# Chunked attention in a streaming-encoder layer: bias matmuls on 64 rows, four probability buffers, a new order of scores and products

## The chip, the cores and the metric

One Trainium2 chip, all 8 cores. Each core computes half of one of the four sequences of the batch; even cores run one program (half 0), odd cores the other (half 1). The metric is the device time of the slowest core, in microseconds (us). A core has a matmul engine (TensorE, "PE" in the profile, with its weight loads "PEld"), VectorE (DVE), ScalarE (ACT), GpSimd (POOL) and a queue engine (SP). The granted clock is the share of its full clock that TensorE got. Some executions fall in a slow state, in which cores of a die run at a lower clock.

## The reference, cut to what matters

```python
x = x + 0.5 * swiglu(rmsnorm(x), ffn1)            # feed-forward, width 2816
z = rmsnorm(x) @ w_in                             # q, k, v (8 heads of 64), conv input (2 x 512)
# chunk of 64 queries attends to its own chunk and the 8 before it (576 keys)
s = einsum(q, k) / 8 + rel_bias[clip(distance)]   # masked where the chunk is out of the band
attn_out = softmax(s) @ v
conv_out = silu(layernorm(depthwise_conv(glu(u))))
x = x + concat(attn_out, conv_out) @ w_out
x = x + 0.5 * swiglu(rmsnorm(x), ffn2)
y = rmsnorm(x)
```

x is 4 x 4096 x 1024. The scores are held transposed: keys on the partitions (tiles of 128), queries on the columns. The bias is constant for far keys, so only a band of at most 256 queries per key tile needs a table; the same table carries the mask (-30000).

## The kernel before

The kernel is generated by Python: a scheduler inside it models the time of each engine at build time, picks the next ready piece of work for TensorE, and writes out a fixed order for every engine. An attention *unit* is one head pair (two heads, `e` = 0 and 1) over some key tiles, 1024 or fewer score columns in two PSUM banks. Scores and bias of a unit:

```python
for (r, a, w, o_) in u["lst"]:            # scores: two heads, 64 contraction rows each
    for e in range(2):
        ops.append((e, kslice(...), qT[e * 64:e * 64 + 64, j, ...], o_, w, ...))
for (r, a, w, o_) in u["lst"]:            # bias and mask: identity (128 x 128) times a table
    for e in range(2):
        if r >= 3:
            ops.append((e, ident, cb[:, tb:tb + hi - lo], o_ + lo - a, hi - lo, ("cb",), None))
        if r < nt:
            ops.append((e, ident, mask0, o_ + r * 128 - a, 128, ("cb",), None))
...
pi = nxt("Pb", 2)                         # two probability buffers
act(Pb[:, pi, :, 0:w], src, AF.Exp, 2 * w, ...)
```

The products take V and a block of ones as weights (128 rows, 64 columns), into an output bank and a sum bank. After the last unit of a head pair, ScalarE makes 1/sum by Ln and Exp, and VectorE multiplies. The loop, one unit of scores ahead of the products, with a fresh bank pair for each head pair:

```python
qk(units[0])
for i, u in enumerate(units):
    if i + 1 < len(units):
        yield rdy1
        qk(units[i + 1])
    yield fn            # P ready, and two free banks if this is the head pair's first unit
    pv(u)
    if u["last"]:
        fin1(u)         # Ln, Exp, later the multiply
```

Where the scheduler expects TensorE to wait 0.8 us or more it inserts dummy matmuls ("fillers", 256 columns into a free bank), to keep its clock up:

```python
n = int((gap - 0.3) / (0.25 if P.t["pe"] < 9 else 0.125))
for i in range(n):
    P.op("pe", lambda h: h.matmul(o, lhsT=onesS, rhs=cb[:, B_ONES:B_ONES + 256], ...), 0.118, ...)
```

The softmax here doesn't subtract the row's maximum and nothing guards it: scores larger than these inputs give would overflow.

## Time and profile before

| | before |
|---|---|
| time, median of the first 4 runs (one of them slow) | 1403.45 us |
| spans of the cores in the profile | 1394.2 to 1401.2 us, granted clock 0.992 to 0.997 |
| TensorE busy, core 0 | 1355.6 us, 97% |
| attention on core 0, two windows | 97.7 + 98.4 us |
| half 0: matmuls, form changes, fillers | 9310, 251, 140 |

How to read the profile here: start times of matmuls are exact, but durations overlap, since matmuls are pipelined. The list of groups shows it for the bias (columns: name, shape, count, busy us, mean ns):

```profile
L484 PE MATMUL psA<-cb_sb 128*128 128x128 bf16 x192 | 22.7, 224 | 0.0
L484 PE MATMUL psA<-cb_sb 128*128 128x256 bf16 x88 | 17.5, 281 | 0.0
```

A bias matmul of 128 columns has a mean of 224 ns, yet the next one of the same form starts 56 ns later. What one costs is the distance from start to start, and the cost of an order shows where that distance exceeds what the width explains.

### The profile page before, as it was taken

The page shows a single profiled execution, that of the slowest core. Times are in us where ns is not written, and L with a number is a line of the kernel's source. Part 1 is how long each engine was busy: PE and PEld are TensorE (multiplying, and loading weights), DVE is VectorE, ACT ScalarE, POOL GpSimd, SP SyncE. Part 2 cuts the span into 40 slices and gives each one's busy share as a digit, 9 for nine tenths or more (in the row PEclk, how much of TensorE's full clock was granted, in tenths as well). Part 3 has the DMA queues.
Part 4 walks back from the last instruction along what each step waited for, and adds up shares of the span by engine and source line. Part 5 has one row for each costly group of instructions (what it writes and reads, how often), then busy time and mean ns, then how long its engine had stood idle before and what let it go on. Part 6 is the DMA issues. An engine that isn't in the chain of part 4 may idle for free.

```text
span 1401.2 us, 25261 instructions; the slowest of 8 cores (1394.2 to 1401.2 us)
## 1 busy us (share of the span) xinstructions
PE 1355.6 (97%) x9310; PEld 846.8 (60%) x9310; DVE 484.9 (35%) x906; ACT 444.7 (32%) x839; POOL 255.2 (18%) x302
## 2 busy tenths in 40 slices
PE   7999999999999999999999999999998999999995
PEld 3575566556554565665565766666664467666654
DVE  3332222452643332222365222225344333222225
ACT  3410011342566631001246100225338663100123
POOL 0155000522123120000062000014041201000012
PEclk9999999999999999999999999999999999999998
DMA  8479144136181443243547544452354406244503
GB/s 192 105 145 197 36 80 87 31 98 146 51 163 28 112 73 69 53 87 51 111 140 241 106 77 90 72 96 65 98 125 92 91 2 121 48 78 87 106 1 123
DMA packets 34032, 132.13 MB, mean 94 GB/s; under 512 B 3440, under 2 KB 11760, under 8 KB 26096
## 3 DMA queue, kind: packets, MB, share of 16 engines
q0 software_dynamic: 17856, 93.48, 35.3%
q1 hardware_dynamic: 16048, 36.96, 8.3%
q8 instruction: 78, 1.28, 0.4%
q14 instruction: 50, 0.41, 0.1%
HBM read 196.37 MB, written 18.09 MB: 153 GB/s over the span
## 4 chain that ended last, share of the span: by engine, by line
PE 89%; ACT 3%; DMA 3%; DVE 2%; issue 2%; DVEq 0%; POOL 0%; ACTq 0%; SPq 0%; POOLq 0%
PE psA L484 52%; PE ps L484 37%; ACT dreg L494 2%; DMA ring<-wgu 2%; DVE hT L714 1%; DVE dreg L714 1%; DMA xres<-xin 1%; DVE xres L885 1%; ACT L492 1%; DMA yout<-dreg 0%; DVE dreg L984 0%; PE ps L472 0%; DVEq L240 0%; ACT scr L492 0%; POOL ring L583 0%
## 5 line engine op out<-in xcount | busy, mean ns | idle before, releaser
L484 PE MATMUL psA<-hT,ring 128*128 128x256 bf16 (+2 forms) x4608 | 718.3, 317 | 5.4 <-DVE hT L714 1.8
L484 PEld LDWEIGHTS psA<-hT,ring 128*128 128x128 bf16 x4608 | 449.5, 98 | 269.7 <-issue 15.3
L494 ACT ACTIVATE dreg<-psA 128x512 f32<-128x512 f32 (+5 forms) x372 | 210.9, 573 | 693.9 <-PE psA L484 688.0
L484 PE MATMUL ps<-at,ring 128*128 128x256 bf16 (+2 forms) x2112 | 327.2, 317 | 0.5 <-DVE xres L885 0.5
L855 DVE TENSOR_TENSOR at<-psA,dreg 128x256 bf16<-128x256 f32 (+2 forms) x264 | 141.5, 536 | 485.6 <-PE psA L484 417.5
L484 PEld LDWEIGHTS ps<-at,ring 128*128 128x128 bf16 x2112 | 206.4, 98 | 119.2 <-issue 0.9
L885 DVE SCALAR_TENSOR_TENSOR xres<-ps,xres 128x256 f32<-128x256 f32 (+2 forms) x192 | 101.8, 533 | 194.4 <-PE ps L484 194.0
L662 POOL TENSOR_TENSOR ssum<-ssum,sq 128x256 f32<-128x256 f32 (+2 forms) x114 | 107.1, 940 | 216.2 <-ACT sq L494 213.3
L583 POOL DMA_DIRECT2D ring<-wgu x45 | 27.7, 616 | 419.1 <-PE psA L484 195.7
L484 PE MATMUL ps<-dreg,ring 128*128 128x256 bf16 (+3 forms) x672 | 97.0, 301 | 0.2 <-DMA ring<-cwscr 0.2
L494 ACT ACTIVATE sq<-xres 128x256 bf16<-128x256 f32 (+2 forms) x115 | 58.0, 511 | 97.8 <-DVE xres L885 64.2
L484 PEld LDWEIGHTS ps<-dreg,ring 128*128 128x128 bf16 x672 | 65.5, 98 | 27.6 <-issue 0.9
L714 DVE SCALAR_TENSOR_TENSOR hT<-xres,cs_sb,rstd 128x256 bf16<-128x256 f32 (+2 forms) x120 | 70.0, 636 | 16.8 <-ACT rstd L494 16.8
L484 PE MATMUL ps<-hT,ring 128*128 128x256 bf16 (+2 forms) x384 | 61.6, 317 | 0.1
L484 PEld LDWEIGHTS ps<-hT,ring 128*128 128x128 bf16 x384 | 37.1, 98 | 21.2 <-issue 0.3
L484 PE MATMUL ps<-dreg,at 128*64 128x256 bf16 (+3 forms) x264 | 35.0, 280 | 12.5 <-ACT dreg L494 12.3
L492 ACT ACT_TABLE_LOAD x36 | 46.2, 1283 | 0.7
L484 PE MATMUL ps<-dreg,cb_sb 128*64 128x256 bf16 (+5 forms) x314 | 42.7, 283 | 1.4 <-DVE dreg L763 1.1
L1356 DVE TENSOR_TENSOR xres<-ps,xres 128x256 f32<-128x256 f32 (+2 forms) x48 | 25.7, 535 | 31.6 <-PE ps L484 31.3
L494 ACT ACTIVATE dreg<-dreg 128x256 f32<-128x256 f32 (+6 forms) x52 | 26.6, 511 | 30.1 <-DVE dreg L984 27.5
L484 PE MATMUL psA<-cb_sb 128*128 128x128 bf16 (+1 forms) x280 | 35.5, 242 | 0.0
L1375 POOL TENSOR_TENSOR dreg<-cmp_sb,cb_sb 128x2304 bf16<-128x2304 bf16 x8 | 32.3, 4042 | 12.9 <-DMA cwscr<-dreg 12.3
(73 smaller groups left out, 568.4 us busy)
## 6 DMA issues: line engine op xcount, KB each, us to landing
ring<-wgu POOLq DMA_DIRECT2D x43, 1024.0 KB, 8.9
ring<-wdA POOLq DMA_DIRECT2D x16, 768.0 KB, 8.8
ring<-wdB POOLq DMA_DIRECT2D x16, 640.0 KB, 6.8
ring<-cwscr POOLq DMA_DIRECT2D x16, 576.0 KB, 5.9
cwscr<-dreg SPq DMA_DIRECT2D x8, 576.0 KB, 9.9
ring<-wab POOLq DMA_DIRECT2D x8, 512.0 KB, 7.6
ring<-wout POOLq DMA_DIRECT2D x4, 1024.0 KB, 9.7
yout<-dreg SPq DMA_DIRECT2D x2, 2048.0 KB, 6.9
```

What stands on the lines that cost most here:

```text
L484: P.op("pe", lambda h: h.matmul(o, lhsT=lhsT, rhs=rhs, start=start, stop=stop, skip_group_check=True), (max(n / 2400.0 + 0.0025, 0.03) if ...
L492: P.op("act", lambda h: h.activation(out=scr[0:1, i:i + 1], in_=onesS[0:1, 0:1], func=func), 1.5, ("cb1",), ())
L494: P.op("act", lambda h: h.activation(out=out, in_=in_, func=func, **kw), 0.12 + n / 1200.0 + (0.09 * sum(isinstance(v, bass.AP) for v in k ...
L583: P.dma("pool", lambda h, dst=dst, src=src: h.dma_start(out=dst, in_=src), wtok(p, i), (256 if p.reads else 512) * w, reads=p.reads, after ...
L662: pool(lambda h: h.tensor_tensor(out=ss, in0=ss, in1=sqt, op=ALU.add), n, (sk, ("sq", i)), (sk,))
L714: dve(lambda h, dst=dst, xin=xin, gcol=gcol: h.scalar_tensor_tensor(out=dst, in0=xin, scalar=gcol, in1=rt, op0=ALU.mult, op1=ALU.mult), n, ...
L855: dve(lambda h, at=at, ub=ub, tt=tt: h.tensor_tensor(out=at, in0=ub, in1=tt, op=ALU.mult), n, (("ps", bU), ("tmpF", ti)), (("AT", gi, fl, ...
L885: dve(lambda h, xo=xo, bk=bk: h.scalar_tensor_tensor(out=xo, in0=bk, scalar=0.5, in1=xo, op0=ALU.mult, op1=ALU.add), n, (("ps", b), xk), ( ...
L1356: dve(lambda h, xo=xo, bk=bk: h.tensor_tensor(out=xo, in0=bk, in1=xo, op=ALU.add), n, (("ps", b), xk), (xk,))
L1375: P.op("pool", lambda h, o_=o_, i0=i0: h.tensor_tensor(out=o_, in0=i0, in1=i1, op=ALU.mult), 4.1, ("cmp", "cb"), (("cwb", i % 2),))
```

## The change

Intent: make TensorE's attention work cheaper and let it run further ahead of ScalarE. Four things change together. (1) The bias is multiplied as two halves of 64 table rows, with 64-row identity windows, so both heads of a pair run side by side in the array form of the scores. (2) Four probability buffers instead of two, up to four units open, and a loop that picks scores or products one at a time. (3) One output and sum bank pair for the whole attention of a group, instead of a fresh one per head pair; the other two banks stay free for projections. (4) The conv's squares are kept in place and summed in one run of 16 matmuls. The rest is memory moved about to make room; for that, the ones of the sum products share a block that holds 1/1024, which Ln undoes by a scale of 1024.

```diff
-                            for e in range(2):
-                                hh = 2 * j + e
-                                if r >= 3:
-                                    ...
-                                    ops.append((e, ident, cb[:, tb:tb + hi - lo], o_ + lo - a, hi - lo, ("cb",), None))
-                                if r < nt:
-                                    ops.append((e, ident, mask0, o_ + r * 128 - a, 128, ("cb",), None))
+                            parts = []
+                            if r >= 3:
+                                q0 = (r - 4) * 128
+                                for half_, lim in ((0, 192), (1, 256)):
+                                    lo, hi = max(a, q0), min(a + w, q0 + lim)
+                                    parts.append((half_, B_BT + j * BW + 192 * half_ + lo - q0, o_ + lo - a, hi - lo))
+                            if r < nt:
+                                parts.append((0, B_M0, o_ + r * 128 - a + 64, 64))
+                            for half_, tb, c_, w_ in parts:
+                                for e in range(2):
+                                    z = B_ID + 64 * (1 - half_)
+                                    ops.append((e, cb[64 * e:64 * e + 64, z:z + 128], cb[64 * e:64 * e + 64, tb:tb + w_],
+                                                c_, w_, ("cb",), w_ / 4800.0 + 0.0025))
 ...
-                        pi = nxt("Pb", 2)
+                        pi = nxt("Pb", 4)
 ...
-                        if u["bi"] == 0:
-                            del ob[:]
-                            for e in range(2):
-                                ob.append(fb_take())
-                                mode["lru"].remove(ob[e])
 ...
-                    qk(units[0])
-                    for i, u in enumerate(units):
-                        ... (the loop above)
+                    def qk_at():
+                        if a == N or a - c > 3:
+                            return INF
+                        ...
+                    while c < N:
+                        fn = lambda: min(qk_at(), pv_at())
+                        yield fn
+                        while True:
+                            lim = ...
+                            if pv_at() <= lim and units[c]["last"]:
+                                pv(units[c]); fin1(units[c]); c += 1
+                            elif qk_at() <= lim:
+                                qk(units[a]); a += 1
+                            elif pv_at() <= lim:
+                                pv(units[c]); ...; c += 1
+                            else:
+                                break
```

(The first products of a head pair now wait until the multiply of the one before has read the single bank pair.)

## The prediction

> **What bounds the kernel now.** I read the page's engine shares first, then the chain that ended last, then the sums of waits, then two stretches of the timeline.
>
> ```profile
> PE 1355.6 (97%) x9310; PEld 846.8 (60%) x9310; DVE 484.9 (35%) x906; ACT 444.7 (32%) x839; POOL 255.2 (18%) x302
> PE 89%; ACT 3%; DMA 3%; DVE 2%; issue 2%; DVEq 0%; POOL 0%; ACTq 0%; SPq 0%; POOLq 0%
> ```
>
> TensorE sets the end: it is busy 97% of the span and is 89% of the chain. Most of that is the two feed-forward layers, which the change doesn't touch. Only TensorE time saved, or TensorE waits shortened, can move the result. Attention runs twice on a core, once per group of blocks; on core 0 its matmuls lie at 370 to 468 us and 1049 to 1147 us. Two windows around them, and the list of TensorE's waits:
>
> ```profile
> 370.00:468.00 98.00, 92.26 (x798) 49.21 (x797) 49.33 (x78) 67.55 (x103) 19.93 (x18) 1.00 0.36 69
> 1048.00:1147.00 99.00, 90.91 (x874) 51.20 (x873) 42.35 (x74) 72.83 (x112) 17.30 (x16) 0.98 0.32 65
> ```
>
> ```profile
> PE ps L484 <- ACT dreg L494: 13.0, 28, 3.0
> PE ps L472 <- DVE dreg L763: 7.0, 1, 7.0
> ```
>
> The columns of the windows are length, then PE, PEld, DVE, ACT and POOL busy. ScalarE is 69% and 74% busy here, against 32% over the span, and 13.0 us of TensorE's waits are the product with V waiting for the exponential. So in attention ScalarE is the second limit. The pipeline itself, TensorE then ScalarE:
>
> ```profile
> 393.96 0.39 PE L484 MATMUL psA<-dreg,at 64*128 64x512 bf16 x2
> 394.28 0.39 PE L484 MATMUL psA<-cb_sb 128*128 128x256 bf16 x2
> 394.61 0.30 PE L484 MATMUL ps<-dreg,at 128*64 128x256 bf16 x2
> 394.74 0.28 PE L484 MATMUL ps<-dreg,cb_sb 128*64 128x256 bf16 x2
> 394.95 0.39 PE L484 MATMUL psA<-dreg,at 64*128 64x384 bf16 x4
> ```
>
> ```profile
> 1082.02 0.41 PE L484 MATMUL ps<-dreg,at 128*64 128x512 bf16 x2 [0.20 <-ACT dreg L494]
> 1089.34 0.41 PE L484 MATMUL ps<-dreg,at 128*64 128x512 bf16 x2 [0.19 <-ACT dreg L494]
> ```
>
> ```profile
> 1082.90 0.50 PE L484 MATMUL psA<-cb_sb 128*128 128x256 bf16 x4
> 1083.50 1.02 ACT L494 ACTIVATE dreg<-psA 128x1024 bf16<-128x1024 f32 x1 [0.71 <-PE psA L484]
> 1084.82 1.02 ACT L494 ACTIVATE dreg<-psA 128x1024 bf16<-128x1024 f32 x1 [0.29 <-PE psA L484]
> 1086.05 1.02 ACT L494 ACTIVATE dreg<-psA 128x1024 bf16<-128x1024 f32 x1 [0.20 <-PE psA L484]
> ```
>
> In the first of these three, the start times matter: the durations of matmuls overlap. A unit of attention runs in three array forms: scores (64 rows by 128), bias (128 by 128, an identity as the weights), products and sums (128 by 64). The score pair of 512 columns holds TensorE from 393.96 to 394.28, 0.32 us, where 512 columns take 0.216 us between equal forms. I took the distances from start to start of all matmuls of core 0: with the same form after it, a full-array matmul of 128, 256, 512 columns holds the array 56, 109, 216 ns (medians); with another form after it, 152, 205, 312 ns. So each change of form costs 96 ns at every width. The last two fences are one head pair in a stretch with nothing else to run: it takes 7.32 us, and ScalarE, itself nearly full, still idles 0.71 + 0.29 + 0.20 us waiting for scores, because only one unit of scores is computed ahead.
>
> **What the Trainium skill says.** "TensorEngine Tiling (Array Packing)", Key Properties: changing the tiling mode drains the engine, changing only the tile does not. The trace agrees, 96 ns a change. The same page's Performance Considerations allow two-fold row tiling when the contraction is 64 or less; the score pairs show it (two matmuls of 64 rows start 3 to 4 ns apart and share one stream time). "TensorE: Matmul & The Clock Gate", Back-to-back issue gap: N/2.4 + 2.5 ns when warm; 56, 109 and 216 ns agree. The same section says that small matmuls stop getting shorter at about 25 ns each; the kernel before has no matmul under 128 columns, so no trace of it shows this, and the change adds 64-column ones.
>
> **The change, part by part.** Counts below are from the order of the two built programs; half 0 is the program of cores 0, 2, 4, 6, half 1 of the odd cores.
>
> Fewer form changes. The bias now uses 64-row matmuls, the same form as the scores, and the new order issues several units of scores and of products in a row. Changes of form fall from 251 to 156 in half 0 and from 240 to 140 in half 1: 95 x 0.096 = 9.1 us and 100 x 0.096 = 9.6 us less.
>
> Bias work. Before, half 0 has 280 bias matmuls on the full array, 192 of 128 and 88 of 256 columns: 192 x 0.056 + 88 x 0.109 = 20.3 us. After, there are 456, in 228 pairs (two heads side by side): 72 pairs of 64 columns, 68 of 128, 44 of 192, 44 of 256. Score pairs followed by score pairs in the trace take 64 ns at 128 and 117 ns at 256 columns, so about N/2.4 + 10. That gives 72 x 0.037 + 68 x 0.064 + 44 x 0.090 + 44 x 0.117 = 16.1 us, 4.2 less. The 37 ns is extrapolated; at the 50 ns of two issue floors it would be 0.9 us more, so I count 3.2 us saved (half 1: 19.9 to 15.1, counted as 3.8).
>
> Keep-warm fillers. The program puts dummy 256-column matmuls where its schedule expects TensorE to wait 0.8 us or more. They run whether or not the wait comes. Half 0 goes from 140 to 204, half 1 from 214 to 271, all the new ones in attention: 64 x 0.109 = 7.0 us and 57 x 0.109 = 6.2 us more. This is the sign that a good part of the saved TensorE time becomes waiting for ScalarE.
>
> Other waits. I summed, over each attention stretch of core 0, what the start-to-start distances exceed width plus form change: 7.4 and 11.6 us, fillers not counted; on core 1, 4.9 and 9.8 us. Scores may now run up to four units ahead (four probability buffers instead of two), score and product matmuls are picked one unit at a time, and the output projection of a finished block is spread between units instead of coming as one burst of 64 matmuls. In the lonely stretch the 1.2 us of ScalarE idling per head pair should fall. Against it: the output and sum banks were a fresh pair per head pair and are now one pair for all, so the first product of a head pair waits for Ln (0.59 us), Exp (0.63) and the multiply (0.69) of the one before. I put the net at 6 us less of 19.0 in half 0 and 5 less of 14.7 in half 1; this is a judgement, not a sum.
>
> Moved only. The 16 matmuls of the conv's squares per group stand together at the end instead of between; same form, same columns. Exponentials, Ln and evictions keep their counts and sizes. Smaller tables in the setup lie before TensorE needs them.
>
> Sum, half 0: -9.1 - 3.2 + 7.0 - 6 = -11.3 us; half 1: -9.6 - 3.8 + 6.2 - 5 = -12.2 us. The even cores were the slower, so 1403.45 - 11.3 = 1392; as the interleaving may well give more than I dared in the judged term, I say 1391.
>
> **The rivals.** First, ScalarE is the true bound of attention, and all TensorE time saved comes back as waits for the exponential. For it: 72.83 us of ScalarE in the second window, and the added fillers. Against it: outside the lonely stretches TensorE had projections to run, and was busy 91 to 92 of 98 to 99 us. It would leave 1400 to 1404. Second, the single output pair puts Ln, Exp and multiply, about 1.9 us, on the path at each of the 24 head pairs of half 0 (six blocks of four). With 1 us exposed at half of them, 12 us eat the gain: about 1403. Against it: up to three units of exponentials can be ready meanwhile. Third, the overlap works fully: form changes and bias save 12.3 us, fillers only replace waits, and 12 of the 19 us of waits go: about 1384. Fourth, 64-column pairs or their weight loads cost far more than 37 ns; at 100 ns, 72 x 0.063 = 4.5 us are lost.
>
> **Range and chances.** The certain part (changes of form, bias) is 12 to 13 us; fillers and waits can add or remove about 10. So 1380 to 1400 should hold it 8 times in 10. Two per cent is 28 us, down to 1375.4; that needs the certain part and nearly all of attention's waits, which ScalarE's load forbids: 0.04. A loss over 2% would need waits doubled: 0.01.
>
> **What would show it.** Right: form changes at 96 ns each still, 95 fewer; bias groups as 64*128 forms whose pairs follow each other in 40 to 120 ns; both attention windows of core 0 shorter by 4 to 8 us each, the rest of the span unchanged within 1 us; ScalarE's share in them higher, up to 80%. Wrong: fillers followed by waits of over 1 us at the start of each head pair (the second rival); bias pairs of 64 columns spaced over 60 ns; or waits on ScalarE adding up to over 20 us. If the time falls but the feed-forward stretches changed, my account of the cause is wrong even where the number is right.

## The result, and the profile after

The changed kernel takes 1387.21 us (median of 10 runs) against 1404.67 us (median of 15 runs of the kernel before, slow ones included in both medians). The ratio of the fast runs is 0.9886, 95% interval 0.9875 to 0.9897: some 16 us less. A ratio here is the mean time of one kernel's fast runs over that of the other's of the same rounds, so it is not quite the ratio of the medians. Spans by core are 1377.4 to 1382.6 us in the profile. On a second chip, as a control for later runs, it measured 1387.14 against 1402.90, ratio 0.9893 (0.9880 to 0.9906).

The page of the changed kernel, engine shares and chain by engine:

```profile
PE 1342.8 (97%) x9550; PEld 849.4 (61%) x9550; DVE 484.6 (35%) x901; ACT 447.6 (32%) x847; POOL 256.5 (19%) x302
PE 85%; DMA 6%; ACT 3%; DVE 2%; issue 2%; POOL 0%; SPq 0%; DVEq 0%; ACTq 0%; POOLq 0%
```

TensorE is as busy in share, with 240 more matmuls and 12.8 us less busy time. The two attention windows of core 0, in the columns of the windows shown in the prediction:

```profile
368.00:454.00 86.00, 84.15 (x892) 48.29 (x890) 43.83 (x68) 68.06 (x106) 18.90 (x17) 1.00 0.42 78
1040.00:1129.00 89.00, 86.12 (x1017) 54.40 (x1016) 39.41 (x66) 71.61 (x112) 17.15 (x16) 1.00 0.35 73
```

From the first score matmul to the end of the last product, attention went from 97.7 and 98.4 us to 85.2 and 87.4, so 12 and 11 us less, with about the same ScalarE work in the windows (68.06 and 71.61 us, against 67.55 and 72.83), so ScalarE is busy 79% and 80% of them. The matmuls that were three forms per unit, now from the timeline of TensorE:

```profile
403.36 0.39 PE L482 MATMUL psA<-dreg,at 64*128 64x256 bf16 x4
403.59 0.38 PE L482 MATMUL psA<-cb_sb 64*128 64x64 bf16 x6
403.90 0.35 PE L482 MATMUL ps<-dreg,at 128*64 128x384 bf16 x2
```

The four scores (two pairs of 256 columns) hold the array 0.23 us and the bias follows with no change of form. The six bias matmuls, 512 columns per head, hold it 0.31 us: 0.213 of streaming and one change of 0.096. And three lines of the list of TensorE's waits over the span:

```profile
PE psA L482 <- DVE hT L712: 4.0, 5, 1.0
PE ps L482 <- DVE dreg L1283: 2.0, 6, 0.6
PE psA L482 <- ACT dreg L492: 1.1, 3, 0.4
```

The line of 13.0 us, products waiting for the exponential, is gone from the list. Two others stand there: the first product of a head pair waits for the multiply of the one before (L1283, 2.0 us), and, after attention, the second feed-forward waits for its normalised input (L712; 4.0 us, 1.8 before).

To split the result I took the two attention windows of core 0 (first score matmul to the end of the last product) apart. Projections, attention work, form changes and fillers are counted from the order of the built program and multiplied by the spacings of the trace: columns/2.4 + 2.5 ns for a full-array matmul, columns/4.8 + 3 ns for one of a side-by-side pair, 96 ns for a change of form, 109 ns for a filler. Counting from the built order matters, since the traces of some cores lack about 100 matmul records. Waits are the rest of the window, so they include what is lost while the granted clock is low.

| core 0, us | windows | projections | attention work | form changes | fillers | waits | rest of the span and projections |
|---|---|---|---|---|---|---|---|
| before | 196.1 | 75.4 | 71.0 | 23.9 (249) | 4.7 | 21.1 | 1280.5 |
| after | 172.6 | 73.6 | 65.8 | 14.8 (154) | 11.7 | 6.7 | 1283.7 |
| difference | | | -5.2 | -9.1 | +7.0 | -14.4 | +3.2 |

The sum is -18.5 us; the span of core 0 fell by 18.6. On core 1 the same terms are -5.8, -9.6, +6.3, -9.2 and -0.7: -19.0, and its span fell by 18.9.

Part of these waits is a lower clock. After the longest wait of the kernel before, the trace has a stretch of 3.4 us at half clock (the third column from the right), in which TensorE is busy throughout:

```profile
1073.26 0.41 PE L484 MATMUL ps<-dreg,at 128*64 128x512 bf16 x2 [2.96 <-ACT dreg L494]
1073.83:1077.24 3.41, 3.41 (x26) 1.57 (x24) 0.00 (x0) 1.23 (x2) 0.00 (x0) 0.50 0.48 124
```

Half of it, 1.7 us, is an estimate of what it cost; it sits in the 21.1 us of waits, and the windows of the changed kernel have no such stretch. So the gain has a small share that comes by way of the clock.

### The profile page after: what moved, and what is told of

The parts are those of the page before. It is cut to its first block, busy times and chain, and to the rows that moved or that the text cites. A ratio compares the mean times of both kernels' runs of the same rounds, so it can differ in the third digit from the quotient of the medians.

```text
span 1382.6 us, 25718 instructions; the slowest of 8 cores (1377.4 to 1382.6 us)
## 1 busy us (share of the span) xinstructions
PE 1342.8 (97%) x9550; PEld 849.4 (61%) x9550; DVE 484.6 (35%) x901; ACT 447.6 (32%) x847; POOL 256.5 (19%) x302
## 3 DMA queue, kind: packets, MB, share of 16 engines
q0 software_dynamic: 17856, 93.48, 36.2%
## 4 chain that ended last, share of the span: by engine, by line
PE 85%; DMA 6%; ACT 3%; DVE 2%; issue 2%; POOL 0%; SPq 0%; DVEq 0%; ACTq 0%; POOLq 0%
PE psA L482 51%; PE ps L482 34%; DMA ring<-wgu 3%; ACT dreg L492 1%; DVE dreg L712 1%; DVE hT L712 1%; DMA xres<-xin 1%; DMA ring<-wv 1%; ACT L490 1%; ACT pb L492 1%; DMA yout<-dreg 0%; DMA ring<-cwscr 0%; DMA dreg<-gscr 0%; DVE xres L883 0%; DVE dreg L1283 0%
## 5 line engine op out<-in xcount | busy, mean ns | idle before, releaser
L492 ACT ACTIVATE dreg<-psA 128x256 f32<-128x256 f32 (+4 forms) x330 | 173.6, 530 | 670.6 <-PE psA L482 662.6
L492 ACT ACTIVATE sq<-xres 128x256 bf16<-128x256 f32 (+2 forms) x115 | 57.8, 511 | 98.4 <-DVE xres L883 64.9
L712 DVE SCALAR_TENSOR_TENSOR hT<-xres,cs_sb,rstd 128x256 bf16<-128x256 f32 (+2 forms) x120 | 73.4, 660 | 5.2 <-ACT rstd L492 5.2
L492 ACT ACTIVATE dreg<-dreg 128x288 bf16<-128x288 f32 (+8 forms) x84 | 40.3, 480 | 59.6 <-DVE dreg L1111 29.4
L492 ACT ACTIVATE pb<-psA 128x1024 bf16<-128x1024 f32 (+2 forms) x42 | 37.6, 911 | 3.9 <-PE psA L482 3.9
L1393 POOL TENSOR_TENSOR dreg<-pb 128x2304 bf16<-128x2304 bf16 x8 | 32.2, 4040 | 4.7 <-DMA cwscr<-dreg 4.2
L470 PE MATMUL ps<-cb_sb 128*128 128x256 bf16 x204 | 26.6, 283 | 6.3 <-issue 6.3
L482 PE MATMUL ps<-ring,hT 128*128 128x512 bf16 x136 | 30.9, 379 | 0.6 <-DMA ring<-wv 0.6
```

The costliest lines, as they stand in the source:

```text
L482: P.op("pe", lambda h: h.matmul(o, lhsT=lhsT, rhs=rhs, start=start, stop=stop, skip_group_check=True), (max(n / 2400.0 + 0.0025, 0.03) if ...
L492: P.op("act", lambda h: h.activation(out=out, in_=in_, func=func, **kw), 0.12 + n / 1200.0 + (0.09 * sum(isinstance(v, bass.AP) for v in k ...
L712: dve(lambda h, dst=dst, xin=xin, gcol=gcol: h.scalar_tensor_tensor(out=dst, in0=xin, scalar=gcol, in1=rt, op0=ALU.mult, op1=ALU.mult), n, ...
L1393: P.op("pool", lambda h, o_=o_, i0=i0: h.tensor_tensor(out=o_, in0=i0, in1=i1, op=ALU.mult), 4.1, ("cmp", "i32", "cb"), (("cwb", i % 2),))
```

## The experiments

Two theories. A: TensorE's work is what counts, so cheaper bias and fewer changes of form are the gain. B: attention is paced by the exchange between TensorE and ScalarE, so TensorE time saved alone comes back as waiting, and the deeper order is the gain. Part (3), the single bank pair, is a suspect for a loss. Every run below gave a correct result unless said otherwise, and its ratio is to the kernel before on the same chip. Every edit makes the generator write a new fixed order, with another number of fillers; so a run tests an edit with the order that comes of it, not the edit alone.

**1. The new bias alone, in the kernel before** (bias_only).

```diff
 # kernel before; loop, two probability buffers and bank pairs unchanged
-    ops.append((e, ident, cb[:, tb:tb + hi - lo], ...))       # full array
+    ops.append((e, cb[64*e:64*e+64, z:z+128], cb[64*e:64*e+64, tb:tb+w_], ...))   # 64 rows, two halves
```

> The kernel before with the new bias alone (64-row bias matmuls and tables); old attention loop, two probability buffers, output pair per head pair. Built order: form changes 251 to 188 in half 0, 240 to 181 in half 1; fillers 140 to 172 and 214 to 291. Theory A (TensorE work is what counts: 63 x 0.096 = 6.0 us of form changes and about 4.5 us of bias time come off in full): ratio to before 0.992 to 0.993, some 10 us less. Theory B (ScalarE limits attention, so TensorE time saved alone returns as waits on the exponential): ratio 0.997 to 1.000, and the sum of TensorE's waits on ScalarE plus fillers grows by 6 us or more over the 13.0 us and 43 attention fillers of before.

Measured: 1398.97 against 1402.25 us, ratio 0.9979 (0.9967 to 0.9992). Theory A asked for 0.992 to 0.993 and falls; B's range holds. On core 0 attention work and form changes fell by 11.2 us together, but fillers and waits together rose from 25.8 to 31.8 us. Its list of waits, where before it was 13.0 us:

```profile
PE ps L481 <- ACT dreg L491: 14.5, 24, 3.5
```

TensorE is ready sooner and waits longer for the same exponential. Over half of the saving is given back. (Core 0's span fell by 6.9 us, the time of the slowest core by only 3: the other even cores have clocks of 0.990 to 0.992 here, against 0.992 to 0.994 before.)

**2. The old bias in the changed kernel** (old_bias). The bigger tables leave room for three probability buffers only, so its control is run 3.

```diff
 # changed kernel with three probability buffers
-    ops.append((e, cb[64*e:64*e+64, z:z+128], cb[64*e:64*e+64, tb:tb+w_], ...))
+    ops.append((e, ident, cb[:, tb:tb + hi - lo], ...))
```

> The changed kernel with the old full-array bias (identity weights, one matmul per head and key tile), new attention loop and one output pair; for want of memory three probability buffers instead of four, so it is to be compared with three_p. Form changes 233 and 223. Theory A (form changes and bias time are the gain): at most 2 to 4 us of the 16 us remain, ratio 0.997 to 0.999. Theory B (overlap by the new loop is the gain): 10 us or more remain, ratio 0.990 to 0.993.

Measured: 1396.18 us, ratio 0.9956 (0.9940 to 0.9971), some 6 us less than before: between the two expectations. So the loop alone (with the single bank pair and the conv's squares, which stay in) is not the gain either. It did do what B says to the waits: in core 0's attention, fillers and waits fell from 25.8 to 14.8 us, and the exponential is no longer waited for by products.

```profile
PE ps L485 <- DVE dreg L1282: 2.2, 4, 0.8
PE psA L485 <- ACT dreg L495: 1.4, 3, 0.7
```

**3. Three probability buffers** (three_p), the control of run 2.

```diff
-                        pi = nxt("Pb", 4)
+                        pi = nxt("Pb", 3)
-                        if a == N or a - c > 3:
+                        if a == N or a - c > 2:
```

> The changed kernel with three probability buffers and at most three open units instead of four; the control for old_bias. Form changes 168 and 160, fillers 201 and 281. If the fourth buffer matters little: ratio to before 0.989 to 0.991 (the changed kernel has 0.9886). If depth is the gain: 0.993 or more.

Measured: 1385.47 us, ratio 0.9881 (0.9866 to 0.9896), the same as with four. No worth of the fourth buffer shows. Now the two halves can be added up: bias alone -0.21%, loop without the new bias -0.44%, together -1.19%. Part (4), the conv's squares, was not run alone. The parts are worth more together than apart. In the old loop the new bias saved 11.2 us of core 0's TensorE work and gave 6.0 of them back as idle time; in the new loop (runs 2 and 3) it saved 11.5 and gave back 2.7.

**4. Two probability buffers** (two_p).

```diff
-                        pi = nxt("Pb", 4)
+                        pi = nxt("Pb", 2)
-                        if a == N or a - c > 3:
+                        if a == N or a - c > 1:
```

> The changed kernel with two probability buffers and at most two open units, as before. Form changes 198 and 185, fillers 307 and 332, that is 103 and 61 more fillers than in the changed kernel (11 and 7 us). Theory B: with the single output pair and no depth, the chain Ln, Exp, multiply is exposed at each head pair, ratio 0.998 to 1.004. Theory A: only 42 form changes come back (4 us), ratio 0.991 to 0.993.

Measured: 1405.06 us, ratio 1.0022 (1.0008 to 1.0035). The whole gain is gone, though bias and most of the saved form changes are still there. As theory B said, the wait that replaces the exponential is the multiply of the head pair before, through the single bank pair:

```profile
PE ps L482 <- DVE dreg L1283: 6.3, 12, 1.0
PE ps L482 <- ACT dreg L492: 3.0, 9, 0.5
```

With the fillers that stand in those waits (22.9 us), core 0's attention idles 36.2 us, more than before the change (25.8) and twice as much as with three buffers (17.5, from runs 2 and 3).

**5. The single bank pair alone, in the kernel before** (one_pair).

```diff
 # kernel before
-                        if u["bi"] == 0:
-                            ... take two free banks
-                            mode["lru"] += b2          # given back after the multiply
+                    # one pair taken at the start of the group's attention; the first products of a
+                    # head pair wait for the multiply of the one before (cut; their priority rule goes too)
```

> The kernel before with one output and sum bank pair for all head pairs, as in the changed kernel, and nothing else; one unit of scores ahead as before. Built order: fillers 140 to 265 and 214 to 296 (125 and 82 more, 13.6 and 8.9 us). If the single pair is a cost that only depth hides: attention windows longer, ratio 1.004 to 1.010. If the single pair is free (it leaves two banks to other work): 0.998 to 1.001.

Measured: 1406.85 against 1402.03 us, ratio 1.0035 (1.0020 to 1.0051), just under the range expected of a cost. Taken alone the single pair loses some 5 us; a wait that the list of the kernel before doesn't have appears:

```profile
PE ps L484 <- DVE dreg L1291: 4.9, 9, 0.8
```

So this part of the change is a cost. As far as the lists of waits tell, the depth hides most of it, and 2.0 us of it, plus fillers, are left in the changed kernel. That is not shown by a run of its own: a version with depth and two bank pairs was not tried, since with four of the eight banks holding scores and four outputs, none is left for the projections that fill TensorE.

**6. No fillers in attention** (no_fill).

```diff
-                if gap < 0.8 or gap > 100 or "cb1" not in P.lastw:
+                if gap < 0.8 or gap > 100 or "cb1" not in P.lastw or attention_is_running:
```

> The changed kernel without fillers in attention (half 0: 204 to 97). If fillers only stand in waits: the removed 107 x 0.109 = 11.7 us come back as waits on ScalarE and the ratio to before stays 0.987 to 0.990. If fillers overshoot the waits and delay work: 0.983 to 0.986. If the waits without them let the granted clock drop: more half-clock stretches and 0.990 to 0.994.

Measured: 1390.95 us, ratio 0.9914 (0.9899 to 0.9929), slower than the changed kernel by 0.3% (by 0.2%, with intervals that overlap a little, if its second measurement, 0.9893, is taken; neither was on this chip). The fillers stand in waits: without them core 0's waits are 20.5 us, against 6.7 + 11.7 with them. The list of waits says on what, and the list of cores why it is slower:

```profile
PE ps L483 <- DVE dreg L1284: 7.0, 7, 1.8
PE psA L483 <- ACT pb L493: 3.7, 2, 3.5
```

```profile
core 1: 1386.6 us, clock 0.990
core 7: 1384.3 us, clock 0.990
```

In the changed kernel these two cores had clocks of 0.997 and 0.995. Over all fast runs the cores have 0.989 to 0.994, against 0.993 to 0.998 in the changed kernel. The gaps bring stretches of half clock, as the third reading said. On core 1 one of 10 us surrounds the end of a wait for an exponential that stands behind the Silu block:

```profile
423.25 0.42 PE L483 MATMUL ps<-dreg,vh 128*64 128x256 bf16 x2 [6.19 <-ACT dreg L493]
421.00:431.00 10.00, 6.84 (x56) 3.77 (x58) 0.69 (x1) 7.99 (x10) 0.00 (x0) 0.51 1.03 183
```

On core 0, 6.8 us of attention run at half clock, so some 3.4 of the 20.5 us are that and not waiting. The run also shows what the changed kernel really waits for: the multiply (7.0 us), and score banks behind the Silu block on ScalarE (3.5 us in one wait).

**7. No Ln and Exp of the sums, in the changed kernel** (no_ln). The result is wrong (relative error 0.035): the multiply uses a constant.

```diff
-                        act(rs[:, ri, 0:n], bank(b2[1])[:, 0:n], AF.Ln, n, ..., scale=1024.0)
-                        act(rt, rt, AF.Exp, n, (("rs", ri),), (("rs", ri),), scale=-1.0)
...
-                            dve(lambda h: h.tensor_tensor(out=o_, in0=i0, in1=rt, op=ALU.mult), n, ...)
+                            dve(lambda h: h.tensor_scalar(out=o_, in0=i0, scalar1=1.0 / 600, ...), n, ...)
```

> The changed kernel without Ln and Exp of the softmax sums (24 x 1.2 us less for ScalarE and a chain shorter by as much); wrong result on purpose, the multiply uses a constant. Theory B (waits on ScalarE are what is left in attention): the 11.6 us of fillers and 6.7 us of waits of core 0 fall by 6 to 10 us, ratio to before 0.981 to 0.985. If attention is TensorE-bound already: 0.987 to 0.989.

Measured: 1377.01 us, ratio 0.9815 (0.9800 to 0.9830), 0.7% under the changed kernel: as expected of waits on ScalarE (across chips: the changed kernel was not run on this one). Fillers and waits of core 0 fall from 18.4 to 8.8 us. The run takes away both ScalarE's load and the chain to the multiply, and does not tell these two apart.

**8. The same removal in the kernel before** (no_ln_before), wrong as well.

> The same removal in the kernel before; wrong result on purpose. With two output pairs and one unit ahead, if its waits come from ScalarE's load: 5 to 9 us less, ratio 0.994 to 0.996. If they come from the order (TensorE waits for the one exponential in flight, whatever else ScalarE does): ratio 0.997 to 1.000.

Measured: 1386.50 against 1402.03 us, ratio 0.9889 (0.9874 to 0.9904). This is far more than either reading expected. The products' wait for the exponential, 13.0 us in the kernel before, is nearly all gone:

```profile
PE ps L484 <- ACT dreg L494: 1.6, 5, 0.7
```

The list of the kernel before has no wait for the multiply, so it is ScalarE's work on Ln and Exp that made the products wait for the exponential; whether by its amount or by its place in the queue, the run does not tell. The gain is as large as that of the change, but it is not the same 16 us: run 7 shows that the removal is still worth some 10 us on top of the change, so only about 6 of the 16 us are common to both (an estimate: 16 + 16 alone, 26 together).

**9. The changed kernel again, and a candidate beyond it** (after_again, silu_once, sq_dve, sq_silu, on one chip). Run 6 showed a wait behind the Silu of the conv's norm. They run as two blocks of eight, each with a table load before and after it; one block of 16 saves two loads. The other edit moves the squares of the third norm to VectorE while attention runs.

```diff
 # silu_once
-                    if grp % 8 == 0:
-                        yield lambda: max(P.est("act", (("acc", grp + 7),)) - 0.2, P.t["act"] - 1.0)
+                    if grp == 0:
+                        yield lambda: max(P.est("act", (("acc", 15),)) - 0.2, P.t["act"] - 1.0)
 # sq_dve: during attention
-                act(sqt, xin, AF.Square, n, ...)
+                dve(lambda h: h.tensor_tensor(out=sqt, in0=xin, in1=xin, op=ALU.mult), n, ...)
```

> The changed kernel itself, unedited, on the same chip as the next three, as their control: ratio to before 0.988 to 0.990.

> The changed kernel with the 16 Silu of the conv norm in one run instead of two runs of eight with two exponentials between: two table loads of 1.28 us and their dummy fewer per group on ScalarE. If ScalarE's load in attention is what is left: 21 and 39 fillers fewer, 2 to 4 us less, ratio to before 0.985 to 0.987. If the longer block of Silu (about 8 us without an exponential) starves TensorE: 0.989 or more.

> The changed kernel with the squares for the third norm on VectorE instead of ScalarE while attention runs (about 11 us per group off ScalarE, VectorE was about half busy). These squares come late, where the output projection already fills TensorE, and the count of fillers does not change (206, 271): if only the load in the lonely stretch counts, ratio to before 0.987 to 0.990, no gain; if ScalarE's load counts everywhere in attention: 0.981 to 0.985.

> Both edits together, the candidate for a better version: as silu_once by the first reading (0.985 to 0.987), 0.980 to 0.983 if both count.

| | median, us | ratio to before | 95% interval |
|---|---|---|---|
| after_again | 1387.14 | 0.9893 | 0.9880 to 0.9906 |
| silu_once | 1386.11 | 0.9867 | 0.9852 to 0.9882 |
| sq_dve | 1386.89 | 0.9888 | 0.9873 to 0.9904 |
| sq_silu | 1383.70 | 0.9860 | 0.9843 to 0.9877 |

The squares on VectorE gain nothing, although they take some 17 us of ScalarE's work out of core 0's windows (150.7 to 133.9 us, durations summed). That fits the first reading: ScalarE's load counts only where nothing else can feed TensorE, and these squares come later. It is not shown, since the edit also loads VectorE, which makes the multiply: the wait for it was 2.0 us in after_again and is

```profile
PE ps L482 <- DVE dreg L1289: 3.0, 5, 1.6
```

The longer Silu block gains about 0.26% over the changed kernel, with intervals that still touch. (In its profile core 0 waits 6.0 us for the output projection's weights, in two waits on a DMA that after_again and sq_silu don't have, and is the slowest core.) Both together are 0.33% under it, with intervals apart: the lowest time that gave a correct result, on three fast runs, but not to be told from silu_once.

## Why the prediction was right

The time lies in the range (1387.2 in 1380 to 1400) and "within 2%" was right. Of the size, 16 us were measured and 12 predicted. That the range held owes something to its width: on core 0 two terms missed by 2.8 and 7.6 us in one direction and one by 3.2 in the other. Point by point:

- **Form changes, 95 x 96 ns:** right, though the prediction misreads its source: 152, 205 and 312 ns are about the medians of all forms together. Those of full-array matmuls alone are 195, 220 and 309, since many of their changes contain a wait; the undisturbed ones take 149 to 152, 202 to 205 and 309, so 93 to 96 ns more than 56, 109 and 216. In the changed kernel's trace a 256-column matmul is still followed after 205 ns by another form and after 109 ns by its own.
- **Bias work, 3.2 us:** too small. The pairs were charged N/2.4 + 10 ns, and 64-column pairs more. In the trace after, bias pairs followed by bias pairs take 28, 56, 83 and 109 ns at 64, 128, 192 and 256 columns. That gives 72 x 0.028 + 68 x 0.056 + 44 x 0.083 + 44 x 0.109 = 14.3 us instead of 16.1 and 0.9 of allowance, so 6.0 us were saved. The extra 10 ns had come from scores followed by scores (66 and 120 ns from pair to pair, 2 to 3 more than the prediction states), and bias pairs don't have them. The fourth rival, costly 64-column pairs, is out.
- **Fillers, +7.0 us:** right as a count. But they are waits in another dress, and the prediction's own term for waits has to be read with them: run 6.
- **Other waits, -6 us:** mis-sized; the split gives -14.4 on core 0 (0.8 of it belongs to the bias, since both kernels were split with one formula) and -9.2 on core 1. Of the 14.4, some 1.7 us are the half-clock stretch (the same on core 1). The line of products waiting for the exponential is gone from core 0's list. That line alone proves little: it is down to 3.0 and 2.2 us in runs 4 and 5 too, which have no depth, because fillers stand in the waits, and without fillers core 1 waits 6.19 us for one exponential (run 6). Fillers and waits together show what depth does: 36.2 us with two open units, 17.5 with three. Run 8 shows what had stood behind the wait: ScalarE's work on Ln and Exp.
- **Signs:** both windows fell by 12 and 11 us, more than the 4 to 8 named, and ScalarE's share in them rose to 80%, as said. Bias pairs of 64 columns are 28 ns apart, below the 40 to 120 named.
- **Rest of the span unchanged within 1 us:** wrong on core 0, +3.2 us (core 1: -0.7). The prediction called a change there a sign that its account is wrong; as it is a loss, it cannot be where the gain comes from. Part of the gain is given back right after the first attention, where the last norms now finish later and the second feed-forward waits for them. These waits have no counterpart at the same place before:

```profile
490.02 0.38 PE L482 MATMUL psA<-hT,ring 128*128 128x256 bf16 x2 [0.80 <-DVE hT L712]
491.38 0.82 PE L482 MATMUL psA<-hT,ring 128*128 128x256 bf16 x6 [0.97 <-DVE hT L712]
```

  That the later, spread output projection is the cause is argued from the order and not tested.
- **First rival (ScalarE bounds attention, all comes back):** true in the larger part of the bias alone (run 1), false of the whole, because the loop changed with it. **Second rival (the single bank pair eats the gain):** a real cost, 5 us alone (run 5); with two buffers the multiply leads the waits of attention and the whole gain is gone (run 4). Depth hides it, as far as the waits tell. **Third (overlap works fully, 1384):** nearest to what happened, 1387. The prediction gave each part its own sum and so missed that they are worth more together than apart.

## What to carry to other kernels

When two engines hand work to each other through few buffers, a saving on one of them can be worth little until the order lets it run ahead (here 0.21% of the time in the old loop, 0.75% in the new one); make depth and savings together, and test each alone to see which one pays. Count changes of the array form in the built order, since each had a fixed price in these traces, and arrange small side matmuls in the form of their neighbours. Fillers hide waits in a profile: add them to the waits before saying that an engine is busy.

## What the Trainium skill lacked or had wrong

- "TensorEngine Tiling (Array Packing)", Key Properties, says that changing the mode drains the engine and gives no price. Here it is 96 ns a change at 128, 256 and 512 columns alike, on both kernels.
- "TensorE: Matmul & The Clock Gate", Back-to-back issue gap, puts the start-to-start floor at about 25 ns for 1 to 64 columns, without saying that this is not per matmul between row tiles. Two 64-row matmuls of 64 columns side by side took 28 ns for the pair, start of pair to start of pair (48 cases), and most partners start about 4 ns apart. These 4 ns stand elsewhere on the same page, in its part on packing small matmuls.
- The same page says that idle gaps lower the clock. The runs agree. No page has dummy matmuls as a remedy, or what they are worth: taking 107 and 142 fillers per core out of attention (11.7 and 15.5 us of dummy matmuls) cost 0.2 to 0.3%, with granted clocks of 0.990 to 0.994 instead of 0.994 to 0.997.
